# Background transfers asked for by GpSimd, and another spread of the background work, in a two-block transformer kernel

## The chip, the cores and the metric

The kernel runs on one core of a Trainium2 chip. The metric is the time of one execution in microseconds (us) on the device, the median of several runs. The engines of a core work side by side, each through its own list of instructions in order: TensorE (PE; its weight loads are shown as PEld), VectorE (DVE), ScalarE (ACT), GpSimd (POOL) and SyncE (SP). SyncE computes nothing here: it asks for transfers between the device memory and the on-chip memory. [...]

## The reference

256 tokens of width 1024 pass through two blocks. All numbers are 32-bit floats.

```python
mod = (silu(c) @ w_mod + b_mod).reshape(1, 6, 1024)        # block 1; also with c_ctx for a context
h = rmsnorm(x) * (1 + scale) + shift                       # shift, scale: rows of mod
x = x + mod[2] * token_mixers(h)                           # gated recurrence and a spatial gate
x = x + mod[5] * swiglu(modulated rmsnorm(x))              # feed-forward
# block 2, twice: a modulation of its own, a mixer, and a retrieval among 16384 experts
mod = silu(c_2) @ mod_w_2[l] + mod_b_2[l]                  # six rows of 1024 per layer l
x = x + g1 * (gla_mixer(h) if l == 0 else sliding_window_attention(h))
x = x + g2 * peer(h)                                       # layer l = 0, 1
# between them: a third modulation (two rows) for shared keys and values
def peer(h):       # 8 heads, 16 experts each, found by product keys
    u = u_tab[e]; a = gelu(einsum('pd,phkd->phk', h, u))
    return einsum('phk,phkd->pd', softmax(scores) * a, v_tab[e])
```

What matters here: every modulation row needs a product of one vector (silu(c) or silu(c_2)) with a 1024 x 1024 weight matrix. There are 20 rows; two are made at the start on TensorE, the others in the background.

## The kernel before

**Weights.** Nearly all time goes into matrix products whose weights stream in from device memory, in half-tiles of 128 x 1024 floats (512 KB). For each, `halves` (L258) asks SyncE for the transfer into a buffer `raw` (L218), lets ScalarE round it to `wh` (L263), and VectorE make the rest `wl` = raw - wh (L265); TensorE then multiplies three times (activation high x wh, high x wl, low x wh: L279, L280, L281 and the like). `raw` is a ring of 4 buffers, `wh` and `wl` are rings of 3; some stages add to them (`more`, L223; buffers `rawx`, `whx`, `wlx`).

**Stages.** In order: the first block's mixers (weights w_in, w_pa, w_pb, w_o), its feed-forward (w_up, w_down), the GLA mixer (gla_in, gla_out), the first retrieval (peer 0), the attention mixer, the second retrieval (peer 1). A retrieval goes over all experts: a loop over the key table (`u_pair`, L1607, 128 half-tiles), then one over the value table (`v_pair`, L1715, 128 half-tiles; per half-tile, 4 products of 512 columns, each threefold: 12 matmuls; 2 x 128 tokens by 2 x 512 columns are collected in four PSUM banks).

**Background pieces.** A modulation row is cut into 8 pieces; `mod_piece` (L373) makes one: a transfer of 512 KB of weights, and one VectorE instruction that multiplies them by the row `crow` and sums over it (L390, with a read-out of the sum); the eighth piece adds the bias (L394), and for a gate row GpSimd writes the 1024 results to device memory (L398). Pieces are handed out by a credit: after each half-tile `pump` (L413) adds `rate`, and a piece is made at each full unit. So a rate of 0.3 is three pieces in ten half-tiles. `need` (L419) makes the pieces that are missing at once. The rates are set for the stages in `program` (L1813): m_rate and m2_rate (first block), f_rate (feed-forward), g_rate (GLA); in the value loop of peer 0 it is 0.56 (L1845). The names of the pieces' weights are w_m (also for the two modulations of the second block) and w_kv.

**Where a piece's weights land.** In the first stages `raw` serves (L381, L220), and the piece takes a place in the ring between the weights. In the value loop of peer 0 there is a buffer of its own, named RO (set in L1695, dropped at the 37th pair of half-tiles, L1737): `mod_fetch` (L366) asks for the next piece's weights as soon as the piece before is in the order (L391), so one transfer is always under way. RO exists once. After that pair, `raw` serves again.

**Order.** The program is written in one sequence; a planner puts each engine's instructions in an order of its own before the run, by its estimates of durations. At run time every engine goes strictly through its order, and waits where something is not ready.

Of the kernel before, what the change touches and what calls it, by code (L numbers as in the profile page):

```python
# [111 lines left out]
class Prog:  # L112
# [253 lines left out]
    def mod_fetch(s):  # L366

        if s.bg and s.mnext is None and s.mraw_at:
            key, part, k = s.bg[0]
            s.mnext = s.t(s.mraw_at[0], [128, 1024], tag=s.mraw_at[1], bufs=1)  # L370
            s.nc.sync.dma_start(s.mnext, s.a["w_" + key][part - s.part0[key], k])

    def mod_piece(s):  # L373

# [1434 lines left out]
def program(ctx, tc, a, parts="1g0sf"):  # L1809
    s = Prog(ctx, tc, a)  # L1810
    x = s.setup()
    s.route_rate = 1.2
    s.m_rate, s.m2_rate, s.f_rate, s.g_rate = 0.3, 0.7, 0.7, 0.0  # L1813
    pre = ExitStack()
    if parts[0] == "1":
        def more():
            s.add_mods("m", range(2, 6))
            s.rate = s.m_rate
            if "g" in parts:
                s.add_mods("m0", range(5))  # L1820
        s.more_mods = more
        first = s.block1(x, "g" in parts)
    else:
        s.ectx.close()
        prep = s.pool("pre", 1, ctx=pre)
    if "g" in parts:
        if parts[0] == "g":
            s.add_mods("m0", range(5))
            s.drain()
            first = s.enter(x, s.gla_entry(x, s.scratch(prep)), None)  # L1830
            pre.close()
        first = s.gla(x, first, "0" in parts)
    if "0" in parts:
        if parts[0] == "0":
            s.add_mods("m0", range(3, 5))
            s.drain()
            first = s.enter(x, s.peer_entry(0, x, s.scratch(prep)))
            pre.close()
        s.add_mods("m0", [5])
        s.u_rate, s.v1_rate, s.v_rate, s.peer_need = 0.0, 0.0, 0.25, ("m0", 5)  # L1840
        if "s" in parts:
            s.rope_setup()
            s.add_mods("kv", range(2))
            s.add_mods("m1", range(5))
            s.u_rate, s.v1_rate, s.v_rate = 0.0, 0.56, 0.56  # L1845
            s.peer_need = "m1", 4
        first = s.peer(0, x, first, "swa" if "s" in parts else "store")
    if "s" in parts:
        if parts[0] == "s":
            s.rope_setup()  # L1850
            s.add_mods("kv", range(2))
            s.add_mods("m1", range(5))
            s.drain()
            s.kvctx = ExitStack()
            first = s.enter(x, s.swa_entry(x, s.scratch(prep), s.pool("kv", 1, side="right", ctx=s.kvctx)))
            pre.close()
        first = s.swa(x, first)
        s.add_mods("m1", [5])
        s.u_rate, s.v1_rate, s.v_rate, s.peer_need = 0.0, 0.0, 0.2, ("m1", 5)
        s.peer(1, x, first, "final" if "f" in parts else "store")  # L1860
    if parts[-1] in "1g":
        s.store_x(x)
    s.actx.close()
# [61 lines left out]
def build(arrays, parts="1g0sf"):  # L1925
    import concourse.bacc as bacc
    nc = bacc.Bacc("TRN2", target_bir_lowering=False, num_devices=1)
    aps = {}
    for k, v in arrays.items():
        aps[k] = nc.dram_tensor(f"in_{k}", v.shape, mybir.dt.from_np(v.dtype), kind="ExternalInput").ap()  # L1930
    aps["out"] = nc.dram_tensor("out_0", (256, 1024), F32, kind="ExternalOutput").ap()
    with tile.TileContext(nc) as tc:
        with ExitStack() as ctx:
            program(ctx, tc, aps, parts)
    return nc
# [8 lines left out]
```

## Time and profile before

| | us |
|---|---|
| median of 3 runs (2369.48 to 2372.11) | 2371.63 |
| the profiled execution | 2373.57 |
| its span | 2371.6 |
| TensorE busy | 2305.4 (97%) |
| VectorE busy | 1844.0 (78%) |
| ScalarE busy | 1162.8 (49%) |
| GpSimd busy | 16.0 (1%) |

The profile is of one execution. "Busy" is the time in which an engine works on instructions; a weight load overlaps the matmuls. A wait is put down to the instruction that released it. The granted clock (PEclk) is 1.0 at TensorE's full level of 2.4 GHz and 0.5 at the lower one, 1.2 GHz. The span leaves out about 2 us that the measured time has around it.

### The profile page before, as it was taken

Reading aid. Unit: us, or ns where it says so; the run is one execution under the profiler, and the core shown is the slowest. Engines: PE = TensorE matmul, PEld = TensorE weight load, DVE = VectorE, ACT = ScalarE, POOL = GpSimd, SP = SyncE. Lnnn points to the kernel's source line nnn. Section 1 sums busy time; section 2 is a strip of 40 time slices with the busy share of each in tenths; the row PEclk is TensorE's granted clock in tenths of the full one; section 3 lists DMA queues with packets and bytes.
Section 4 is the critical chain, followed back from the end, with each engine's and each line's share of the span. In section 5 each row is a group of like instructions: output and inputs, shape, how many; then the busy total and the mean of one; then the engine's idle time right before and its main releaser. Section 6 shows DMA issues by size and latency. Waiting matters only on the chain. (4 is left out here: it accounts for less than half of the span.)

```text
span 2371.6 us, 39890 instructions
## 1 busy us (share of the span) xinstructions
PE 2305.4 (97%) x15360; PEld 2046.5 (86%) x15360; DVE 1844.0 (78%) x3502; ACT 1162.8 (49%) x1893; POOL 16.0 (1%) x32
## 2 busy tenths in 40 slices
PE   8999999989999999999999999999999999999998
PEld 6978889977899999998777787589999999888886
DVE  5689878777679989997777877558997999556665
ACT  4464444464455444445444555555454445445543
POOL 0000000000000000000000000000000000000000
PEclk8999999999999999999999999999999999999999
DMA  7647599744445544448888983144554445656772
GB/s 297 200 125 268 201 351 328 279 137 154 136 162 193 162 157 155 155 152 265 267 272 297 346 313 135 45 162 162 186 165 156 152 152 169 192 187 224 239 230 99
DMA packets 130590, 475.97 MB, mean 201 GB/s; under 512 B 15056, under 2 KB 15824, under 8 KB 129120
## 3 DMA queue, kind: packets, MB, share of 16 engines
q1 hardware_dynamic: 130208, 473.41, 59.0%
q8 instruction: 120, 1.97, 0.3%
q14 instruction: 70, 0.57, 0.1%
q0 software_dynamic: 192, 0.02, 0.0%
HBM read 472.30 MB, written 1.07 MB: 200 GB/s over the span
## 5 line engine op out<-in xcount | busy, mean ns | idle before, releaser
L265 DVE TENSOR_TENSOR wl<-raw,wh 128x1024 fp32r<-128x1024 f32 x426 | 519.7, 1222 | 133.7 <-ACT wh L263 132.9
L263 ACT ACTIVATE wh<-raw 128x1024 fp32r<-128x1024 f32 x426 | 448.3, 1054 | 289.3 <-PE psB L1616 114.6
L1615 PE MATMUL psB<-acth,wh 128*128 128x256 f32 x1776 | 503.6, 284 | 1.4 <-ACT u L1621 1.4
L1617 PE MATMUL psB<-acth,wl 128*128 128x256 f32 x1776 | 500.1, 282 | 0.0
L1616 PE MATMUL psB<-actl,wh 128*128 128x256 f32 x1776 | 499.6, 281 | 0.0
L280 PE MATMUL psA<-wl,acth 128*128 128x512 f32 x880 | 350.9, 399 | 6.8 <-DVE wl L265 6.7
L279 PE MATMUL psA<-wh,acth 128*128 128x512 f32 x880 | 349.3, 397 | 2.8 <-ACT acth L563 2.4
L281 PE MATMUL psA<-wh,actl 128*128 128x512 f32 x880 | 348.8, 397 | 0.5 <-DVE actl L564 0.5
L1615 PEld LDWEIGHTS psB<-acth,wh 128*128 128x128 f32 x1776 | 334.6, 188 | 1.8 <-ACT u L1621 1.8
L1617 PEld LDWEIGHTS psB<-acth,wl 128*128 128x128 f32 x1776 | 334.7, 188 | 0.4 <-DVE wl L265 0.4
L1616 PEld LDWEIGHTS psB<-actl,wh 128*128 128x128 f32 x1776 | 334.7, 188 | 0.0
L1710 ACT ACTIVATE acth<-u 128x256 fp32r<-128x256 f32 x240 | 98.2, 416 | 273.6 <-PE psA L280 273.6
L280 PEld LDWEIGHTS psA<-wl,acth 128*128 128x128 f32 x880 | 165.3, 188 | 53.3 <-DVE wl L265 14.8
L279 PEld LDWEIGHTS psA<-wh,acth 128*128 128x128 f32 x880 | 165.3, 188 | 43.4 <-ACT acth L563 2.4
L281 PEld LDWEIGHTS psA<-wh,actl 128*128 128x128 f32 x880 | 165.2, 188 | 40.8 <-DVE actl L564 1.0
L263 ACT ACTIVATE whx<-raw 128x1024 fp32r<-128x1024 f32 x123 | 127.5, 1053 | 78.3 <-PE psB L1616 28.2
L265 DVE TENSOR_TENSOR wlx<-raw,whx 128x1024 fp32r<-128x1024 f32 x123 | 149.2, 1221 | 20.8 <-ACT whx L263 20.5
L1711 DVE TENSOR_TENSOR actl<-u,acth 128x256 fp32r<-128x256 f32 x240 | 99.7, 422 | 61.2 <-ACT acth L1710 61.2
L265 DVE TENSOR_TENSOR wl<-rawx,wh 128x1024 fp32r<-128x1024 f32 x94 | 114.8, 1222 | 37.8 <-ACT wh L263 36.5
L263 ACT ACTIVATE wh<-rawx 128x1024 fp32r<-128x1024 f32 x94 | 98.9, 1056 | 87.1 <-PE psB L1616 42.1
L265 DVE TENSOR_TENSOR wlx<-rawx,whx 128x1024 fp32r<-128x1024 f32 x79 | 96.1, 1222 | 41.6 <-ACT whx L263 41.2
L263 ACT ACTIVATE whx<-rawx 128x1024 fp32r<-128x1024 f32 x79 | 81.9, 1055 | 73.9 <-PE psB L1616 16.1
(559 smaller groups left out, 4582.3 us busy)
## 6 DMA issues: line engine op xcount, KB each, us to landing
raw<-in_peer_v SPq DMA_DIRECT2D x222, 512.0 KB, 5.1
raw<-in_peer_u SPq DMA_DIRECT2D x211, 512.0 KB, 3.9
rawx<-in_w_m SPq DMA_DIRECT2D x55, 512.0 KB, 6.2
raw<-in_w_m SPq DMA_DIRECT2D x48, 512.0 KB, 6.0
rawx<-in_peer_u SPq DMA_DIRECT2D x45, 512.0 KB, 4.3
rawx<-in_peer_v SPq DMA_DIRECT2D x34, 512.0 KB, 5.8
rawx<-in_w_up SPq DMA_DIRECT2D x29, 512.0 KB, 6.4
raw<-in_w_in SPq DMA_DIRECT2D x27, 512.0 KB, 4.6
```

The lines of the kernel that those rows point to most:

```text
L263: s.queue(nc.scalar.activation(wh, x, AF.Copy))
L265: s.queue(nc.vector.tensor_tensor(wl, x, wh.bitcast(F32), op=OP.subtract))
L279: mm(out, lhsT=lh, rhs=rh, start=start, stop=False)
L280: mm(out, lhsT=lh, rhs=rl, start=False, stop=False)
L281: mm(out, lhsT=ll, rhs=rh, start=False, stop=stop)
L1615: mm(pu, lhsT=wh[:, sl], rhs=hT[:, k], start=(k == 0), stop=False)
L1616: mm(pu, lhsT=wh[:, sl], rhs=lT[:, k], start=False, stop=False)
L1617: mm(pu, lhsT=wl[:, sl], rhs=hT[:, k], start=False, stop=(k == 7))
L1710: nc.scalar.activation(Wh, W, AF.Copy)
L1711: nc.vector.tensor_tensor(Wl, W, Wh.bitcast(F32), op=OP.subtract)
```

## The change

Two lines. The transfers into the buffer of its own are asked for by GpSimd in place of SyncE, and the four rates of the first stages are others.

```diff
@@ mod_fetch, L371
         if s.bg and s.mnext is None and s.mraw_at:
             key, part, k = s.bg[0]
             s.mnext = s.t(s.mraw_at[0], [128, 1024], tag=s.mraw_at[1], bufs=1)
-            s.nc.sync.dma_start(s.mnext, s.a["w_" + key][part - s.part0[key], k])
+            s.nc.gpsimd.dma_start(s.mnext, s.a["w_" + key][part - s.part0[key], k])
@@ program, L1813
-    s.m_rate, s.m2_rate, s.f_rate, s.g_rate = 0.3, 0.7, 0.7, 0.0
+    s.m_rate, s.m2_rate, s.f_rate, s.g_rate = 0.2, 0.6, 0.6, 0.4
```

In all, 41 transfers leave SyncE's list (904 rows before, 863 now) for GpSimd's (37 before, 78 now). In SyncE's list of before, in the value loop of peer 0, a piece's transfer stands behind every two of the value table:

```order
L371 DMA RO_12459<-in_w_m 128x1024
L220 DMA raw_12613<-in_peer_v 128x1024
L220 DMA raw_12633<-in_peer_v 128x1024
L371 DMA RO_12502<-in_w_m 128x1024
L220 DMA raw_12656<-in_peer_v 128x1024
L220 DMA raw_12676<-in_peer_v 128x1024
```

In the changed kernel the pieces' transfers are in GpSimd's list, one behind the other, and the list of SyncE has only those of the table in this place:

```order
L1460 IOTA u_6405 128x800
L371 DMA RO_12455<-in_w_m 128x1024
L371 DMA RO_12459<-in_w_m 128x1024
L371 DMA RO_12502<-in_w_m 128x1024
L371 DMA RO_12545<-in_w_m 128x1024
L371 DMA RO_12588<-in_w_m 128x1024
```

What moved are the 41 requests alone: in VectorE's list the pieces' products (L390 on RO) stand behind every second `wl` of the value table before and after.

The pieces of the first stages move too. Of the 72 that are made before peer 0, the first block has 28 before and 24 now, the feed-forward 44 and 38, GLA none and 10. In VectorE's list of before, in the middle of GLA (L1125 and L1128 use the matmuls' results for the queries and keys, L1145 is the masked scores):

```order
L265 TENSOR_TENSOR wlx_5805<-raw_5801,whx_5803 128x1024
L1125 SCALAR_TENSOR_TENSOR w_991_5407<-psA_5410,w_974_5324 128x512
L1125 SCALAR_TENSOR_TENSOR w_991_5407<-psA_5411,w_974_5324 128x512
L265 TENSOR_TENSOR wl_5881<-rawx_5877,wh_5879 128x1024
L1128 TENSOR_TENSOR w_992_5408<-psA_5534,w_975_5326 128x512
```

And in that of the changed kernel, in the same place:

```order
L265 TENSOR_TENSOR wlx_5789<-raw_5785,whx_5787 128x1024
L1125 SCALAR_TENSOR_TENSOR w_981_5377<-psA_5380,w_963_5291 128x512
L1125 SCALAR_TENSOR_TENSOR w_981_5377<-psA_5381,w_963_5291 128x512
L390 SCALAR_TENSOR_TENSOR raw_5864,u_5478<-raw_5864,crow_3559 128x1024
L265 TENSOR_TENSOR wl_5871<-raw_5867,wh_5869 128x1024
L1128 TENSOR_TENSOR w_982_5378<-psA_5512,w_964_5293 128x512
```

A piece's product now stands between two steps of the mixer, ahead of a `wl`; its weights come through the ring `raw`.

## Rows read from the trace of the kernel before

**Rows 1.** The page: busy us and share by engine, and the granted clock

```profile
span 2371.6 us, 39890 instructions
PE 2305.4 (97%) x15360; PEld 2046.5 (86%) x15360; DVE 1844.0 (78%) x3502; ACT 1162.8 (49%) x1893; POOL 16.0 (1%) x32
...
PEclk8999999999999999999999999999999999999999
```

**Rows 2.** Table of stretches: from:to, length, then busy us (instructions) by engine

```profile
core 0: us, PE busy (x) PEld busy (x) DVE busy (x) ACT busy (x) POOL busy (x), PEclk, DMA share, GB/s
...
110.00:300.00 190.00, 180.14 (x1200) 159.31 (x1201) 163.03 (x260) 98.91 (x126) 1.73 (x3) 0.97 0.59 201
300.00:481.00 181.00, 178.44 (x1239) 166.72 (x1238) 146.02 (x205) 80.25 (x99) 1.08 (x2) 0.99 0.86 314
481.00:583.00 102.00, 93.98 (x524) 75.18 (x523) 70.57 (x119) 53.11 (x75) 2.27 (x5) 0.98 0.40 132
...
1077.00:1211.00 134.00, 132.85 (x562) 103.82 (x560) 97.29 (x144) 65.48 (x96) 0.56 (x1) 1.00 0.82 268
1211.00:1324.00 113.00, 108.13 (x459) 85.11 (x458) 89.19 (x144) 52.45 (x80) 0.32 (x1) 1.00 0.84 290
...
2010.00:2340.00 330.00, 330.00 (x1421) 266.08 (x1420) 206.51 (x260) 168.43 (x245) 0.56 (x1) 1.00 0.64 210
```

**Rows 3.** All instructions on the tile RO: least/median/most ns, first and last start

```profile
L371 SPq DMA_DIRECT2D RO<-in_w_m x25: 327/328/328, 1076.8 to 1318.4; - x25
L279 PE MATMUL psA<-wh,RO x16: 389/391/504, 1071.0 to 2010.5; 128*128 128x512 f32 x16
L371 SPq DMA_DIRECT2D RO<-in_w_kv x16: 327/328/328, 1122.4 to 1210.4; - x16
...
DMA to landing us min/median/max: 3.5/4.5/6.3
```

**Rows 4.** Waits from 1071 to 1324 us: total us, times, longest

```profile
DVE RO L390 <- DMA RO<-in_w_kv: 27.7, 16, 2.5
DVE RO L390 <- DMA RO<-in_w_m: 25.4, 19, 3.4
PEld psA L280 <- DVE wl L265: 13.8, 21, 1.7
...
PE psA L280 <- DVE wl L265: 5.9, 8, 1.3
```

**Rows 5.** Instructions in order, from 1127 us: start, duration, [idle before <-releaser]

```profile
1128.45 0.08 DVE L390 DVE_READ_ACCUMULATOR RO<-RO,L 128x1 f32 x1
...
1128.56 0.33 SPq L371 DMA_DIRECT2D RO<-in_w_kv  x1
...
1130.03 1.80 SPq L220 DMA_DIRECT2D raw<-in_peer_v  x2
1130.06 0.19 PEld L280 LDWEIGHTS psA<-wl,acth 128*128 128x128 f32 x1 [0.29 <-DVE wl L265]
...
1132.95 1.23 DVE L390 SCALAR_TENSOR_TENSOR RO<-RO,L 128x1024 f32<-128x1024 f32 x1 [1.48 <-DMA RO<-in_w_kv]
...
1134.11 0.08 DVE L390 DVE_READ_ACCUMULATOR RO<-RO,L 128x1 f32 x1
...
1134.22 0.33 SPq L371 DMA_DIRECT2D RO<-in_w_kv  x1
...
1135.69 0.33 SPq L220 DMA_DIRECT2D raw<-in_peer_v  x1
```

**Rows 6.** A GpSimd transfer in order of time; landings of mgate's (GpSimd), of out's (SyncE)

```profile
1122.61 0.16 DVE L394 TENSOR_TENSOR mgate<-mgate,u 128x8 f32<-128x8 f32 x1
...
1123.06 0.56 POOL L398 DMA_DIRECT2D mod<-mgate  x1 [508.76 <-DVE mgate L394]
...
DMA to landing us min/median/max: 2.8/4.6/5.6
...
L1781 SPq DMA_DIRECT2D out<-u x4: 332/362/383, 2359.2 to 2368.0; - x4
...
DMA to landing us min/median/max: 2.0/2.2/2.3
```

**Rows 7.** Stretches around a fall of the granted clock, columns as above; then TensorE's matmuls

```profile
1440.00:1450.10 10.10, 8.05 (x38) 6.13 (x37) 8.76 (x27) 5.56 (x15) 0.00 (x0) 1.00 0.01 2
1450.20:1453.50 3.30, 3.03 (x7) 2.46 (x8) 2.91 (x8) 2.65 (x7) 0.00 (x0) 0.50 0.00 0
...
1451.49 0.63 PE L88 MATMUL psA<-wh,u 128*128 128x512 f32 x1
1451.92 0.63 PE L89 MATMUL psA<-wl,u 128*128 128x512 f32 x1
```

**Rows 8.** The pieces' products of the first stages and their read-outs (line L390)

```profile
L390 DVE SCALAR_TENSOR_TENSOR rawx<-rawx,crow x38: 1215/1219/1224, 73.7 to 463.4; 128x1024 f32<-128x1024 f32 x38
L390 DVE DVE_READ_ACCUMULATOR rawx<-rawx,crow x38: 80/84/89, 74.9 to 464.5; 128x1 f32 x38
```

## The prediction

> **What bounds the kernel now.** I read the page first: its first part for the engines, its second for the course over the span [rows 1]. TensorE is busy for 97% and the granted clock is 0.9 or more nearly throughout, so only its few gaps, or work that opens new ones, can move the end. The table of stretches says where gaps are [rows 2]. From 2010 to 2340 us, the expert-value loop of the second retrieval stage, it is full: 1421 matmuls in 330 us, 0.232 us each. The same loop of the first retrieval stage (first half-tile at 1071 us) has no more products per half-tile, but from 1077 to 1324 us TensorE idles 1.2 + 4.9 us. The difference is the modulation work in it: 41 pieces go through the buffer RO, from 1076.8 to 1318.4 us [rows 3].
>
> The summed waits of that stretch [rows 4] say what is short: VectorE waits 27.7 + 25.4 us for transfers into RO, and TensorE and its weight loads wait for VectorE's `wl`. The instructions in order of time [rows 5] show the chain. RO is a single buffer, so it is a loop: SyncE asks for the transfer at 1128.56; the product over it (L390) starts at 1132.95 after 1.48 us of idling; its read-out ends at 1134.11 + 0.08 = 1134.19; SyncE asks for the next one at 1134.22, 0.03 us later. One loop is 5.66 us. The order of VectorE has one RO product per two `wl`, that is per two half-tiles, which are 24 matmuls, 24 x 0.232 = 5.57 us of TensorE. Over all of it the loop takes (1318.4 - 1076.8)/40 = 6.04 us. So the RO loop, and not TensorE, already sets the pace of this stretch by a little, and VectorE, which works in order, passes each lateness of RO on to the two `wl` behind it.
>
> **The change part by part.** *The transfers into RO.* All 41 leave SyncE's queue for GpSimd's; VectorE's order keeps one RO product per two `wl`. What could be gained is the time by which SyncE was late: 0.03 us per transfer, nothing. The weight transfers behind an RO transfer lose nothing by it and gain nothing: in rows 5 they go out at 1130.03 and 1135.69, right behind the `wl` that frees their buffer, 1.5 us after RO's. GpSimd has hardly anything to do there, so nothing queues ahead on it; behind each RO transfer stands the next one and, once each, the write of a finished gate (L398) and an iota (L633) for a mask, neither of which is wanted soon.
>
> What is added is the price of asking from GpSimd. First the waking: VectorE ends L394 at 1122.61 + 0.16 = 1122.77 and GpSimd's transfer starts at 1123.06, 0.29 us later [rows 6], against SyncE's 0.03: +0.26 us. Then issue to landing. The trace has no large transfer by GpSimd, only six of 4 KB, to landing 2.8/4.6/5.6 us (least, median, most). The nearest of SyncE's are four writes to the same kind of memory, sixty times larger: 2.0/2.2/2.3 us [rows 6]. Per transfer that is 4.6 - 2.2 = 2.4 us more at the medians, 2.8 - 2.3 = 0.5 at least, 5.6 - 2.0 = 3.6 at most. I take 1.9, nearer to the median than to the low end: SyncE's four ran on an idle machine. Below nothing I go by one reason: RO's packets no longer stand in one queue with weight transfers, and its landing on SyncE of 4.5 us at the median has 3.5 as its least [rows 3], so at most 1.0 us could come back. The ends are thus 0.5 + 0.26 - 1.0 = -0.24 and 3.6 + 0.26 = 3.86 us per loop; I take 1.9 + 0.26 = 2.16.
>
> The Trainium skill, page "DMA: Bandwidth & Descriptors", section "Latency and other measured facts", puts the first byte of a transfer from GpSimd at about 1 µs against 0.6 from SyncE. By that the landing would grow by 0.4 us, and the sum would be 40 x (0.4 + 0.26) = 26 us; the six rows are all on the far side of it, and their least is near it.
>
> The sum: 40 loops x 2.16 = 86 us. VectorE has waited for RO 35 times out of 41 (16 + 19) [rows 4]; in the other six it came late itself, and there some 1 us of the addition is covered: -6. That leaves +80. None of it is hidden: TensorE's loop of 5.57 us has no reserve against one of 6.04 + 2.16 = 8.2, and the buffers of `wh` and `wl` hold three half-tiles, already used up at 1130 us, where the weight load waits 0.29 us [rows 5].
>
> TensorE would then stand about 2.6 us in each 8.2. Such a stand can bring its clock down: after the gaps between 1440 and 1450 us, 2 us in 10, the grant fell from 1.00 to 0.50 (1.2 GHz) for 3.3 us [rows 7], with matmuls 0.43 us apart. One such stretch in a loop delays 3.3 x (1 - 0.23/0.43) = 1.5 us of work; 5.57 + 1.5 = 7.1 is still under 8.2, so I cost it at nothing. The cover is the RO loop itself: at two stretches per loop it would be gone.
>
> *The rates of the first stages.* 72 pieces are made before the first retrieval stage, then and now: before 28 beside the first block's mixers, 44 beside its feed-forward and none in the GLA stage; now 24, 38 and 10. Each is 1.22 + 0.08 us of VectorE [rows 8] and one 512 KB transfer. The first block gets 4 x 1.30 = 5 us of VectorE back, the feed-forward 8 us, where TensorE idles 2.6 us of 181 [rows 2] and so has little to give. GLA takes 13 us more in a stage with 70.6 of 102 us busy: it fits on average, but some of the ten stand ahead of steps that TensorE waits for there. I put -3 and +4, together +1, with ends of -6 (TensorE idles 9.9 us from 110 to 300, most of it at fixed joints) and +7 (half of the ten pieces shown in full).
>
> Against the profiled execution, 2373.57 us, this is 2373.6 + 80 + 1 = 2454.6. That one is 1.9 us over the median of the runs; the forecast for the median is 2371.6 + 81 = **2452 us**.
>
> **The rivals.**
> *Small addition.* GpSimd's transfers land at their best, 0.5 us behind SyncE's. For it: one of six was there. Against: the median of six. Then 0.76 x 34 = 26 us: 2398 us. It is also what the page's 0.4 us would give (26 us, above).
> *Not slower.* RO's own queue. The transfer no longer shares SyncE's queue with two weight transfers per loop, lands in its least time, 3.5 us, and that outweighs the waking. It decides if GpSimd's 512 KB land within 4.5 - 0.26 = 4.2 us of issue. Then the waits of TensorE in this stretch go, at most 1.2 + 4.9 = 6 us, and with the first stages the time is 2361 to 2378, say 2367. For it: DMA is 82 to 84% busy here, so queueing is real. Against: a GpSimd transfer of 4 KB took over 4.2 us at the median. The Trainium skill, same page, section "Anatomy of one DMA — SWDGE (gpsimd) path", fits such a transfer as 2.0 us plus its bytes at 436 GB/s, an estimate of 3.2 us here; by that rule this rival is right. The rows of 4 KB, which by it would take 2.0, say 2.8 to 5.6.
> *Much slower.* The top of the range: 3.86 x 40 = 154 us, 2526 us. Or the clock: two stretches at the lower level per loop make TensorE the later one, 5.57 + 3.0 = 8.6, and a loop wholly at it is 24 x 0.43 = 10.3 us against 8.2; ten such loops add 21 us, 2473. For it: a gap every loop. Against: a slow TensorE stops idling, which brings the clock back.
> *The rates alone decide*, since RO is hidden after all: 2366 to 2379. It is part of the second rival.
>
> **How the numbers follow.** Forecast 0.62 (own range 2412 to 2495, 1 to 3 us per loop), small addition 0.16, much slower 0.12, not slower 0.10. About 0.2%, 4.7 us, can be told from no change; the last case splits into 0.05 faster and 0.05 same, the others are all slower: 0.90. The range leaves out the not-slower case, the upper half of the much-slower one and a little of the small addition: 2394 to 2515 us.
>
> **What would show it.** Right: the stretch from the first to the last RO product is about 80 us longer; VectorE's wait for RO grows from 53 to over 120 us; RO issue to landing is over 6 us on GpSimd; TensorE's idle time after `wl` grows by the same amount; the second retrieval stage is only shifted. Step by step: GpSimd starts about 0.3 us after the read-out; GLA's stretch grows by 0 to 7 us and the first block shrinks by as much. Wrong: landing near 4.5 us with no more waiting for RO; or a stretch as long as before because the RO products had slipped behind other work.

## The result and the profile after

The changed kernel takes 2391.22 us (median of 6 runs, 2385.09 to 2393.96), against 2372.42 us of the kernel before (6 runs, 2369.48 to 2374.27): a ratio of 1.0081 [1.0071, 1.0091], some 19 us slower. The direction was forecast, the size was not: 2452 us, with a range from 2394 to 2515.

The page of the changed kernel, its span and its first part, busy us and share by engine, answers to [rows 1]:

```profile
span 2391.2 us, 39920 instructions
PE 2310.5 (97%) x15360; PEld 2045.4 (86%) x15360; DVE 1843.4 (77%) x3502; ACT 1168.2 (49%) x1897; POOL 38.4 (2%) x73
```

The span has grown by 2391.2 - 2371.6 = 19.6 us, and TensorE and VectorE have as many instructions as before (15360 and 3502): GpSimd's added 22 us are the issuing of 41 transfers. Next the instructions on the tile RO (least, median and most ns; first and last start), against [rows 3]:

```profile
L371 POOL DMA_DIRECT2D RO<-in_w_m x25: 537/538/566, 1076.7 to 1323.4; - x25
L279 PE MATMUL psA<-wh,RO x16: 389/389/498, 1070.7 to 2030.5; 128*128 128x512 f32 x16
...
DMA to landing us min/median/max: 3.8/4.2/7.7
```

The 512 KB transfer that GpSimd asks for lands after 4.2 us at the median, where SyncE's took 4.5: 0.3 us sooner, and not 1.9 later. (In the mean of the 41 landings it is 0.07 us sooner, 4.55 against 4.62, since some of GpSimd's come very late.) The loop of RO is (1323.4 - 1076.7)/40 = 6.17 us instead of 6.04, 0.13 more, and not 2.16. The first row of TensorE says where the 19.6 us are. Its first start is that of the first value loop, its last that of the second one (8 of the 16 lie at the start of each): 1071.0 to 2010.5 before, 1070.7 to 2030.5 now. So nothing is lost ahead of the first value loop, and 20.3 us between the two.

The table of stretches (from:to, length, then busy us and instructions of PE, PEld, DVE, ACT, POOL; granted clock, DMA share, GB/s) narrows it down. First the kernel before:

```profile
1077.00:1324.00 247.00, 240.98 (x1019) 188.92 (x1018) 186.48 (x287) 117.93 (x176) 0.88 (x2) 1.00 0.83 278
1324.00:1450.00 126.00, 122.87 (x535) 98.45 (x533) 100.52 (x167) 65.01 (x99) 0.56 (x1) 1.00 0.74 268
```

Then the changed kernel:

```profile
1077.00:1324.00 247.00, 234.90 (x982) 184.14 (x981) 177.88 (x273) 115.23 (x172) 22.68 (x43) 0.99 0.81 275
1324.00:1450.00 126.00, 115.78 (x489) 90.40 (x488) 91.95 (x135) 56.77 (x80) 0.55 (x1) 1.00 0.79 276
```

Up to 1450 us TensorE is 37 + 46 = 83 matmuls behind, at 0.232 us each 19.3 us: nearly the whole loss. The larger share arises after 1324 us, where RO is used once more at most and GpSimd asks for no weights. There the last 17 modulation pieces of this loop (16 before) go through `raw` and `rawx` again, and SyncE asks for them as before. I call this stretch the tail; the prediction had no term for it.

The summed waits of the changed kernel from 1071 to 1466 us (total, times, longest) name what is late in it:

```profile
DVE RO L390 <- DMA RO<-in_w_m: 38.6, 24, 4.4
DVE RO L390 <- DMA RO<-in_w_kv: 29.4, 16, 3.0
...
PE psA L280 <- DVE wl L265: 15.7, 15, 3.9
DVE raw L390 <- DMA raw<-in_w_m: 13.0, 5, 3.9
DVE rawx L390 <- DMA rawx<-in_w_m: 11.0, 3, 4.0
```

In the kernel before the same stretch has one wait of the last kind and none of the one above it:

```profile
PE psA L280 <- DVE wl L265: 6.7, 9, 1.3
DVE rawx L390 <- DMA rawx<-in_w_m: 1.6, 1, 1.6
```

VectorE now stands 13.0 + 11.0 = 24.0 us ahead of products over `raw` and `rawx`. One of them, in order of time, in the changed kernel (start, duration, what; in brackets the idle time before it and what ended it):

```profile
1339.11 1.23 DVE L390 SCALAR_TENSOR_TENSOR raw<-raw,L 128x1024 f32<-128x1024 f32 x1 [1.74 <-DMA raw<-in_w_m]
...
1340.26 1.22 DVE L265 TENSOR_TENSOR wl<-raw,wh 128x1024 fp32r<-128x1024 f32 x1
...
1341.54 0.50 PE L280 MATMUL psA<-wl,acth 128*128 128x512 f32 x1 [1.99 <-DVE wl L265]
```

The product waits 1.74 us for its weights, the `wl` behind it is that much late, and TensorE waits 1.99 us for that `wl`. Why should SyncE's transfers be late when only GpSimd's were touched? The lists say it. VectorE's list in the tail (the `wl` and the product over raw_14432, with what stands between them in the changed kernel), as it is with SyncE asking and the new rates; the dots stand for the product of the piece before, over `rawx`, and in both lists rows of other kinds are left out:

```
L265 TENSOR_TENSOR wl_14353<-raw_14349,wh_14351 128x1024
L265 TENSOR_TENSOR wl_14373<-raw_14369,wh_14371 128x1024
...
L265 TENSOR_TENSOR wl_14396<-rawx_14392,wh_14394 128x1024
L265 TENSOR_TENSOR wlx_14416<-raw_14412,whx_14414 128x1024
L390 SCALAR_TENSOR_TENSOR raw_14432,u_14347<-raw_14432,L_12452 128x1024
```

And in the changed kernel:

```
L265 TENSOR_TENSOR wl_14353<-raw_14349,wh_14351 128x1024
L390 SCALAR_TENSOR_TENSOR raw_14432,u_14347<-raw_14432,L_12452 128x1024
L265 TENSOR_TENSOR wl_14373<-raw_14369,wh_14371 128x1024
L265 TENSOR_TENSOR wl_14396<-rawx_14392,wh_14394 128x1024
L390 SCALAR_TENSOR_TENSOR raw_14455,u_14347<-raw_14455,L_12452 128x1024
```

The same product stands three `wl` earlier. Its request cannot move as far ahead, since it needs a place in the ring. The traces show it: with SyncE asking and the new rates, the requests of the last 14 of these pieces go out 2 to 4 `wl` ahead of their products, mostly 3; in the changed kernel 1 or 2. One `wl` is a half-tile, 12 x 0.232 = 2.8 us, and the transfers land after 5.67 and 5.65 us at the median. So the tail's transfers are no slower than before; the products stand too close behind their requests. Up to the start of the value loop the two lists of VectorE are the same, but for one `wl` that has changed places with two small rows beside it; towards the tail and in it, 21 products over `raw` and `rawx` stand 1 to 4 `wl` earlier, and the last eight over RO 1 or 2. Nothing in the program orders that: the planner chose otherwise once it planned 41 transfers on another engine. That corrects what was said ahead of the run, that the 41 requests alone moved. And it is theory A: the tail's loss is made by the list, and not by who asks.

The part of the loop that uses RO can be split in the same way, since VectorE's lists part only behind the 27th loop of RO, at about 1240 us; ahead of that one pair of neighbouring rows has changed places. The kernel before:

```profile
1077.00:1240.00 163.00, 160.09 (x676) 124.99 (x675) 118.14 (x178) 80.20 (x122) 0.88 (x2) 1.00 0.81 266
1240.00:1324.00 84.00, 80.89 (x345) 63.94 (x344) 68.34 (x110) 37.73 (x55) 0.00 (x0) 1.00 0.87 302
```

The changed kernel:

```profile
1077.00:1240.00 163.00, 158.34 (x668) 123.97 (x667) 116.94 (x177) 77.81 (x119) 15.67 (x30) 1.00 0.78 265
1240.00:1324.00 84.00, 76.56 (x315) 60.17 (x314) 60.94 (x97) 37.43 (x55) 7.01 (x13) 0.96 0.85 293
```

Where the lists are alike, 8 matmuls are lost, 1.9 us; where they differ, 30 in half the time (a matmul on an edge counts in both stretches).

### The profile page after: what moved, and what is told of

Same layout as the page of the kernel before. It is cut to its first block, busy times and chain, and to the rows that moved or that the text cites. A ratio compares the mean times of both kernels' runs of the same rounds, so it can differ in the third digit from the quotient of the medians.

```text
span 2391.2 us, 39920 instructions
## 1 busy us (share of the span) xinstructions
PE 2310.5 (97%) x15360; PEld 2045.4 (86%) x15360; DVE 1843.4 (77%) x3502; ACT 1168.2 (49%) x1897; POOL 38.4 (2%) x73
## 5 line engine op out<-in xcount | busy, mean ns | idle before, releaser
L265 DVE TENSOR_TENSOR wl<-raw,wh 128x1024 fp32r<-128x1024 f32 x422 | 514.2, 1221 | 128.5 <-ACT wh L263 127.7
L1615 PE MATMUL psB<-acth,wh 128*128 128x256 f32 x1776 | 503.6, 284 | 1.6 <-ACT u L1621 1.6
L1615 PEld LDWEIGHTS psB<-acth,wh 128*128 128x128 f32 x1776 | 334.6, 188 | 2.0 <-ACT u L1621 2.0
```

What stands on the lines that cost most here:

```text
L265: s.queue(nc.vector.tensor_tensor(wl, x, wh.bitcast(F32), op=OP.subtract))
L1615: mm(pu, lhsT=wh[:, sl], rhs=hT[:, k], start=(k == 0), stop=False)
```

## The experiments

All ratios are to the kernel before, run beside each on the same chip.

**One part alone: GpSimd asks, the old rates.** From the kernel before:

```diff
-            s.nc.sync.dma_start(s.mnext, s.a["w_" + key][part - s.part0[key], k])
+            s.nc.gpsimd.dma_start(s.mnext, s.a["w_" + key][part - s.part0[key], k])
```

> The engine of the 41 requests changed, the rates of before. Theory A (the other engine reorders the lists behind the RO part, and that is the cost): nearly all of the loss, 15 to 20 us over before, with VectorE waiting 15 to 25 us ahead of the pieces that come through raw, against 1.6 before. Rival B (the rates shift the phase of the pieces in the value loop): within 5 us of before.

Measured: 2385.91 us, 1.0062 [1.0048, 1.0076], +14.4 us, a little under what theory A expected. RO lands after 3.7/4.2/8.8 us, and VectorE waits 19.6 us ahead of the products over `raw` and `rawx`:

```profile
DVE rawx L390 <- DMA rawx<-in_w_m: 12.0, 4, 3.5
DVE raw L390 <- DMA raw<-in_w_m: 7.6, 4, 3.7
```

Most of the loss comes with the change of the asking engine; whether by the asking or by the list, this run cannot tell.

**The other part alone: SyncE asks, the new rates.** From the kernel before:

```diff
-    s.m_rate, s.m2_rate, s.f_rate, s.g_rate = 0.3, 0.7, 0.7, 0.0
+    s.m_rate, s.m2_rate, s.f_rate, s.g_rate = 0.2, 0.6, 0.6, 0.4
```

> The new rates, the requests by SyncE as before. Theory A: -3 to +3 us against before, the value loop of peer 0 as long as before, GLA some 4 us longer and the first block and the feed-forward that much shorter. Rival B: 10 to 20 us slower than before, lost in the value loop.

Measured: 2369.29 us, 0.9991 [0.9983, 1.0], -2.2 us: no change that can be told. The same two waits are 2.3 us together:

```profile
DVE rawx L390 <- DMA rawx<-in_w_m: 1.9, 2, 1.7
DVE raw L390 <- DMA raw<-in_w_m: 0.4, 1, 0.4
```

**The price of asking, by itself.** The prediction took it from the gate rows that GpSimd writes. Here SyncE writes them, in the kernel before:

```diff
-            nc.gpsimd.dma_start(row.rearrange("o (p k) -> (o p) k", k=8), m)
+            nc.sync.dma_start(row.rearrange("o (p k) -> (o p) k", k=8), m)
```

> The kernel before, with the six 4 KB gate writes asked for by SyncE in place of GpSimd. Their landing is looked at. If GpSimd's asking is what made them slow (as the prediction's price had it): 2.0 to 2.6 us at the median. If a write of rows of 32 bytes on a busy machine is slow whoever asks: 3.8 to 5 us. Time within 3 us of before either way.

Measured: 2374.8 us in one run, which tells nothing of the time. The landings do:

```profile
L398 SPq DMA_DIRECT2D mod<-mgate x6: 326/329/392, 117.0 to 2290.7; - x6
DMA to landing us min/median/max: 1.4/3.2/4.7
```

The same six transfers take 3.2 us at the median by SyncE and 4.6 by GpSimd [rows 6]. Neither expectation is met; the median lies between them. So of the 2.4 us by which I compared unlike transfers, 1.4 went with the engine, and 1.0 with the kind of write and what else was under way, as far as six landings tell.

**The tail's products later, GpSimd still asks.** From the changed kernel: from the 31st to the 56th pair of half-tiles, so from the last loops of RO on, a product over `raw` is given out behind the next half-tile's `wl` and tied to it (parts of the edit):

```diff
-            s.queue(nc.vector.tensor_tensor(wl, x, wh.bitcast(F32), op=OP.subtract))
+            il = nc.vector.tensor_tensor(wl, x, wh.bitcast(F32), op=OP.subtract)
+            s.queue(il)
+            while s.pending:
+                s.mod_product(*s.pending.pop(0), after=il)
...
+        if getattr(s, "late", False) and own is None:
+            s.pending.append((r, m, k, key, part, gate))
+            return
```

> The changed kernel, but in the value loop of peer 0 the product of a piece that comes through raw is put behind the wl of the next half-tile, so one or two half-tiles later; requests unchanged. Theory A (VectorE stands before pieces asked for too late): VectorE's wait ahead of these pieces falls from 24 us to under 8 and the time by 8 to 14 us against the changed kernel, to 2377 to 2383. Rival C (the transfers of two queues slow each other and the loss is carried on): less than 4 us of gain.

Measured: 2375.99 us, 1.0022 [1.0011, 1.0033]: by the ratios 14 of the 19 us are gone, by the times 15, so a little more than theory A expected. The two waits fall from 24.0 to 2.8 us, while those for RO stay (L403 is here the line of the product):

```profile
DVE RO L403 <- DMA RO<-in_w_m: 39.2, 24, 4.3
DVE RO L403 <- DMA RO<-in_w_kv: 27.7, 16, 3.0
DVE rawx L403 <- DMA rawx<-in_w_m: 1.6, 1, 1.6
...
DVE raw L403 <- DMA raw<-in_w_m: 1.2, 1, 1.2
```

The stretches show that the tail has recovered in full (540 matmuls, 535 before), and the part ahead of it by 14 of the 37:

```profile
1077.00:1324.00 247.00, 235.88 (x996) 184.83 (x995) 179.67 (x276) 114.38 (x172) 23.04 (x43) 1.00 0.81 274
1324.00:1450.00 126.00, 124.47 (x540) 99.86 (x539) 101.53 (x162) 65.67 (x96) 0.55 (x1) 1.00 0.78 276
```

In the part ahead, too, products over `raw` now stand later, and most of the last ones over RO by one `wl`. What is left there is 23 matmuls, 5.3 us.

**The counterpart: the tail's products earlier, SyncE asks.** This kernel has SyncE and the new rates, and ties the `wl` behind each of the last 20 products over `raw` to it, so that these stand at the very places that they have in the changed kernel. AHEAD is a table of those places; the products over RO stay within one `wl` of where they were. In the expectation, e2 is the kernel with the new rates alone. Parts of the edit:

```diff
-        s.queue(nc.vector.scalar_tensor_tensor(r, r, 1.0, s.crow, op0=OP.mult, op1=OP.mult, accum_out=m[:, k:k + 1]), 0)
+        i = nc.vector.scalar_tensor_tensor(r, r, 1.0, s.crow, op0=OP.mult, op1=OP.mult, accum_out=m[:, k:k + 1])
+        s.queue(i, 0)
+        if s.np in AHEAD:
+            for il in s.wls[AHEAD[s.np]:]:
+                s.follow(il, i)
+        s.np += 1
```

> As e2 (SyncE asks for RO, new rates), but the last 20 modulation pieces of the first value loop that go through `raw` have their products put at exactly the places that they hold in VectorE's order in the changed kernel, 1 to 4 half-tiles earlier than in e2. GpSimd has no part in it. Theory A (it is the order, not the asking engine, that makes VectorE wait for these pieces): VectorE waits 15 to 25 us ahead of products over `raw` and `rawx`, against 2.4 in e2 and 24 in the changed kernel, TensorE waits for `wl` behind them, and the time is 8 to 14 us over e2: 2377 to 2383 us, ratio to before 1.002 to 1.005. Rival C (the waits of the tail come from GpSimd's asking, the order only shifts them): waits under 6 us and a time within 4 us of e2, 2366 to 2373 us, ratio 0.998 to 1.000.

Measured: 2381.76 us, 1.004 [1.0025, 1.0055], 11.6 us more than with SyncE's own list (0.9991 to 1.004 of 2372). VectorE's waits (L395 is here the product) and the two stretches:

```profile
DVE rawx L395 <- DMA rawx<-in_w_m: 13.1, 6, 4.3
...
DVE raw L395 <- DMA raw<-in_w_m: 4.7, 4, 1.9
```

```profile
1077.00:1324.00 247.00, 242.91 (x1024) 189.69 (x1022) 188.95 (x295) 119.06 (x176) 1.44 (x3) 1.00 0.85 285
1324.00:1450.00 126.00, 115.22 (x489) 90.29 (x490) 88.53 (x135) 58.16 (x85) 0.00 (x0) 1.00 0.72 253
```

The tail has 489 matmuls, as in the changed kernel, without a single transfer by GpSimd in it. The rival, that the waits come from GpSimd's asking, falls. Theory A holds in both directions: in the tail the early list costs with either engine, the late one with neither. Ahead of the tail this kernel loses nothing (1024 matmuls, 1019 before); the early places of the products over RO were not tried with SyncE.

**All pieces of this loop by GpSimd.** From the changed kernel. Theory A had at first a narrower form: the requests of the tail's pieces are late because they stand behind weight requests in SyncE's list. Then it should help to take them out of it (`piece` marks a modulation piece):

```diff
-        s.nc.sync.dma_start(r, ap)
+        (s.nc.gpsimd if piece and getattr(s, "late", False) else s.nc.sync).dma_start(r, ap)
```

> The changed kernel, and in the value loop of peer 0 GpSimd asks for the pieces that come through raw as well, so that they no longer stand behind weight transfers in SyncE's list. Theory A (what costs is that these requests go out too late behind weight requests that wait for their buffers): VectorE's wait ahead of these pieces falls from 24 us to under 10, and the time by 6 to 14 us against the changed kernel, to 2377 to 2385. Rival D (the transfers themselves are late, whoever asks, because two queues share the DMA engines): 2388 us or more.

Measured: 2396.65 us, 1.0101 [1.0086, 1.0116]: slower still. The narrower form is wrong. The time is the one that rival D named, but its reason does not show: GpSimd's transfers into `raw` and `rawx` land after 5.4 and 5.6 us at the median, no later than SyncE's in the tail of the changed kernel (5.65). VectorE waits 32.5 us ahead of these products, and GpSimd itself waits, for the ring's buffers to come free:

```profile
POOL raw L220 <- DVE wl L265: 19.0, 7, 10.2
POOL rawx L220 <- DVE wl L265: 18.1, 4, 9.6
DVE rawx L390 <- DMA rawx<-in_w_m: 18.1, 7, 4.2
DVE raw L390 <- DMA raw<-in_w_m: 14.4, 7, 3.7
```

A request can't go out before a `wl` has read the buffer it wants, whoever asks; a product that moves up past other `wl` doesn't bring that moment forward.

**RO in two halves.** SyncE asks, new rates; a piece is two transfers of 256 KB and two products of 512 columns, which should shorten the loop of RO (parts of the edit):

```diff
-            s.nc.sync.dma_start(s.mnext, s.a["w_" + key][part - s.part0[key], k])
...
+            for h in range(2):
+                r = s.t(s.mraw_at[0], [128, 512], tag=s.mraw_at[1] + "2" * h, bufs=1)
+                s.nc.sync.dma_start(r, s.a["w_" + key][part - s.part0[key], k][:, h * 512:h * 512 + 512])
```

> The rates of the change, the requests by SyncE as before, and each RO piece cut into two transfers of 256 KB into two buffers of half the width, with two products of 512 columns and one small addition. If the RO loop sets the pace of this stretch (theory A as the prediction had it): a pair of half-size loops takes under 5.6 us, TensorE's gaps between 1070 and 1320 us go, and the time falls by 3 to 8 us below the kernel with the new rates alone, to 2361 to 2366. Rival E (the loop is not what ends there; VectorE and the landing of the table's weights do): within 2 us of it, or slower by the added VectorE work, 41 x 0.3 us, to 2381.

Measured: 2390.35 us, 1.0071 [1.0059, 1.0084]; both expected times missed. The halves land hardly sooner than whole pieces (4.3 us at the median). The products over RO run from 1074.5 to 1289.6 us, 5.3 us a piece, so under 5.6 as expected; but the planner, again, wrote another list, which gives the 41 pieces 71 half-tiles where they had 83, and TensorE is not faster for it (983 matmuls from 1077 to 1324 us, 1019 before). The tail's list is another one too (L400 is here the product over `raw`):

```profile
DMA to landing us min/median/max: 2.5/4.3/6.6
```

```profile
DVE rawx L400 <- DMA rawx<-in_w_m: 22.5, 8, 4.5
...
DVE raw L400 <- DMA raw<-in_w_m: 15.3, 7, 3.6
```

That is 37.8 us of waiting in the tail with SyncE asking, and a kernel as slow as the changed one. As a test of the loop it settles nothing, since the lists changed with it.

No version is faster than the kernel before by more than can be measured; the new rates alone are level with it.

## Why the prediction was wrong

The sum's large term, the landing of GpSimd's transfers, was mis-sized, and the lists were read at too few places.

- *RO's loop sets the pace of its stretch:* it fits, but no run tests it by itself. VectorE's waits for RO rose from 53.1 us [rows 4] to 38.6 + 29.4 = 68.0. TensorE's side was read a little low: three of the 40 loops have three half-tiles in VectorE's list of before, 83 in all, so 5.78 us a loop and not 5.57.
- *Waking, +0.26 us:* right. In the changed kernel GpSimd starts 0.30 us after the read-out's end (1128.48 + 0.08 to 1128.86):

```profile
1128.48 0.08 DVE L390 DVE_READ_ACCUMULATOR RO<-RO,L 128x1 f32 x1
...
1128.86 0.54 POOL L371 DMA_DIRECT2D RO<-in_w_kv  x1 [4.42 <-DVE RO L390]
...
1133.37 1.22 DVE L390 SCALAR_TENSOR_TENSOR RO<-RO,L 128x1024 f32<-128x1024 f32 x1 [1.86 <-DMA RO<-in_w_kv]
```

- *Issue to landing, "I take 1.9":* this is the step that failed. Measured, it is -0.3 us at the median, and -0.07 in the mean, by which a sum over 40 loops goes; so 40 x (1.9 + 0.07) = 79 us of forecast were not there. The rows from which it came were 4 KB writes by GpSimd on a busy machine against 256 KB writes by SyncE on an idle one. The test of the gate writes leaves 1.4 of that gap of 2.4 us, and none of it carried over to 512 KB loads: the nearest row was one of another kind. From the first to the last RO product it is 246.7 us (1081.2 to 1327.9) instead of 242.5 (1080.7 to 1323.2), and not 80 more. The loop grew by 0.13 us, nearly all of it told by three parts: +0.26 of waking, -0.07 of landing, and -0.08 because VectorE, which before came to the landed weights late now and then, no longer does. What the asking itself costs is cleanest in the first 27 loops of RO, where the lists are alike: 5.89 to 5.94 us a loop, product to product, in the four kernels with GpSimd and whole pieces, and 5.75 to 5.87 in the four with SyncE. That is some 0.1 us at the means, 3 us in 27 loops, so some 4 in 40; the kernel with later products stays 6.7 us behind SyncE with the same rates (2375.99 - 2369.29).
- The Trainium skill, page "DMA: Bandwidth & Descriptors", section "Anatomy of one DMA — SWDGE (gpsimd) path", gives by its fit an estimate of 3.2 us for such a transfer. The measured least is 3.8 and the median 4.2, so it was too low, but nearer than the 4.5 + 1.9 that I took. The Trainium skill, same page, section "Latency and other measured facts", has GpSimd's first byte about 0.4 us behind SyncE's. No row here shows the first byte; the least landings, 3.8 against 3.5, lie the same way, the medians do not.
- *"VectorE's order keeps one RO product per two `wl`":* nearly true where RO is in use, though the last eight stand 1 or 2 `wl` earlier, and I looked no further. The tail's products moved too, and the list is some 12 to 15 us of the 19: 14 to 15 come back when the products over `raw` are put later, 11.6 arise when SyncE's kernel is given the early places. The sum had put this at nothing. The section on the change shows the lists at two places and says that the requests alone moved; the tail was a third place, and its list could have been read before the run.
- *The rates, +1 us (-6 to +7):* -2.2 us, within its bounds, with both parts larger than I had them in the changed kernel. The first matmul of GLA (L1079) starts at 499.9 us instead of 507.5, 7.6 earlier where I had 3; the first of peer 0 (L1615) at 662.8 instead of 663.2, so GLA gives 7.2 back where I had 4. One such price, in the changed kernel: a piece's product stands ahead of a `wl` and of the query and key steps, and waits 4.49 us for its weights.

```profile
535.55 1.23 DVE L390 SCALAR_TENSOR_TENSOR raw<-raw,crow 128x1024 f32<-128x1024 f32 x1 [4.49 <-DMA raw<-in_w_m]
...
541.57 1.23 DVE L265 TENSOR_TENSOR wl<-raw,wh 128x1024 fp32r<-128x1024 f32 x1 [4.79 <-ACT wh L263]
...
544.05 0.66 PE L1135 MATMUL psB<-u,w 128*128 128x128 f32 x4 [3.42 <-DVE w L1129]
```

- *The clock, nothing:* nearly; 0.99 and 1.00 in the two stretches. The grant fell once, from 1.00 to 0.50 for 6.8 us at 1252.0 us, behind a stretch in which TensorE was busy for 4.37 of 6.9 us:

```profile
1245.00:1251.90 6.90, 4.37 (x19) 3.19 (x17) 3.59 (x5) 3.12 (x5) 0.54 (x1) 1.00 0.95 384
1252.00:1258.80 6.80, 5.51 (x13) 4.35 (x14) 5.89 (x11) 0.83 (x2) 0.54 (x1) 0.50 0.91 276
```

  At the prediction's price that is 6.8 x (1 - 0.23/0.43) = 3.2 us of work at most, an estimate; how much of it the loop of RO covered is not shown.
- *The rivals.* "Small addition" (2398 us) came nearest in time, by another way than its own: landings 0.5 us later did not occur. That its time is near is luck. "Not slower" named as its point a landing within 4.2 us, and the median is just that; but TensorE's waits while RO is in use grew where they should have gone, and the tail came on top. "Much slower" had nothing for it.
- What stays open: the two parts alone give +14.4 and -2.2 us, together 12.2, and both at once 18.8. With GpSimd and the old rates TensorE is 39 + 34 = 73 matmuls behind at 1450 us, against 83 with both parts, so the list with both is the worse one by 10 x 0.232 = 2.3 us. Of the other 4 us some may be the spread of executions: ahead of the first value loop the kernel with the new rates alone and the changed one have the same list, and their profiled executions reach that loop at 1066.7 and 1070.7 us. How the 30 matmuls between 1240 and 1324 us divide between the list, the asking and the fall of the clock stays open, and so does on what grounds the planner moves the products.

## What to carry to other kernels

Where a planner writes the lists, an edit to one engine can be an edit to all of them. Compare the lists beyond the place of the edit, and for each instruction that moved up ask when its data can be there: here that was worth 12 to 15 us, and the asking itself some 4 to 7. For the price of an operation that the trace doesn't show, a row of another size and direction is a weak guide. And before an engine is blamed for a wait, give its list to the other engine.

## What the runs showed of the hardware

GpSimd's 512 KB loads, beside SyncE's weight loads at a DMA share of 0.8, landed after 4.1 to 4.2 us at the median in four kernels, and SyncE's own after 4.5 to 4.6 in four others. In the mean there was no such gap (4.55 against 4.62 in the changed kernel and the one before), since GpSimd's latest came after 7.7 to 8.8 us and SyncE's after 6.2 to 6.3. GpSimd began to ask 0.30 us after the read-out that it waited for, SyncE 0.03. Small writes were dearer by GpSimd: 4 KB in 4.6 us against 3.2, at the medians of six. And half the bytes did not halve the time: 256 KB loads by SyncE, asked for in pairs, landed after 4.3 us at the median, 512 KB after 4.5.
